# Gathered expert rows kept in program order, six row buffers, and work and memory moved between stages

## Chip, core and metric

The kernel runs on one core of a Trainium2 chip. The metric is device time in microseconds (us), the median of the runs. A core has a matrix engine (PE, with its weight loads PEld), a vector engine (DVE), a scalar engine (ACT), GpSimd (POOL) and a queue engine (SP) that issues most transfers. Each engine works through its own instruction queue in order, and semaphores connect them.

## The reference, cut to what matters

Two model blocks run one after the other on 512 tokens of width 1024, all in float32. The first block is a mixer (a retention branch and a gated spatial branch) followed by a layer of 16384 experts; every token takes 8 heads x 16 experts:

```python
mod = silu(c) @ w_ada + b_ada
x = x + gate1 * (merged @ w_out)             # the mixer
h2 = modulate(rms_norm(x), shift2, scale2)
# per token and head: the 16 best of 16 x 16 candidate experts, g = softmax of their scores
act = gelu(einsum('td,thkd->thk', h2, peer_u[expert])) * g
x = x + gate2 * einsum('thk,thkd->td', act, peer_v[expert])
```

The second block has two layers with window attention, latent attention and a gated convolution, over the 512 tokens and over 256 context tokens. Each layer takes its modulations as `silu(c_2) @ w_mod_2[l]` for the tokens and `silu(c_ctx_2) @ w_mod_2[l]` for the context. The context path of the second block does not depend on the first block.

## The kernel before

Products in float32 are made of three matmuls in a rounded format: each operand is split into a high part (an ACT copy, line 105) and a low part (a subtraction on POOL or DVE, line 107), and `mm3` issues high x high, high x low and low x high (lines 80 to 82).

The stages, in the order of the program:

- `first_mixer`: weights `wA` come through `next_w`, 256 columns at a time. Modulation vectors are products of a matrix with one vector; `matvec` (line 196) does 128 rows of one on DVE, with a 512 KB load of `wm`. `some(n)`, called by `next_w`, takes n such tasks from `mat_tasks`; the list `mw` holds the pool of the `wm` buffers, their number and n. There are 72 tasks: 32 of the first block's modulation and 40 of the context's.
- `experts`: of the 512 tokens the first 384 (`TD`) go through all experts densely. `up_products` makes their 128 products with `eu` (`wr`, `wl`, `u`, `hb`) and stores `hd`; `route` finds the experts and, in its last part (pool `r3`, lines 835 to 868), builds the matrices of gates `gd`; `context` computes the context path of the second block (`cm`, `wrc`, `wlc`). The down-products (lines 594 to 623) go over 32 groups of four rows of `ev`, with `vr` split into `vh` and `vl`, and `ht` times `gt` split into `ah` and `al`; they accumulate in eight banks. They also do the second block's 48 token-modulation matvecs, two per group, from line 618.
- The last 128 tokens go by gathered rows (`gathered`, line 663): 256 steps, each fetching one 128x1024 tile `sg` by an indirect transfer issued on POOL (line 684). 128 steps are dot products with `htok` on DVE (`matvec`, line 197), and 128 add a weighted row to `sacc` (line 699). A head's additions come 16 steps behind its dot products. `sg` has `SG` = 4 buffers; two rows are fetched ahead, and one more before each step. `sacc` is used at line 635, after the down-products.
- `first_out` ends the first block, normalizes and stores `x`; `second` has the two layers.

The other loops carry the up-products and the gathered steps along. `tick(R)` adds R to a counter and takes an up-product for each whole one; `sparse(S)` does the same for gathered steps. `R1`, `R2`, `R3`, `R4` stand for the two parts of routing, the gate matrices and the context; `S3`, `S4`, `SU`, `S5` for the gate matrices (48 calls), the context's `mm` (its calls follow from the loops), the up-products that are left after it, and each row of the down-products (128 calls).

The framework's scheduler sets the final order of each engine's queue. It goes by readiness and a cost model and not by the order of the program alone: an instruction whose operands are ready may be placed ahead of work that stands before it in the code. Buffers of a pool are reused in turn, and a pool that is opened after another was closed may lie on the same memory, from the left side or, with `side="right"`, from the right; its first writes then wait for the last use of what was there.

```python
for _ in range(SG - 2):
    fetch()
for k, (i, j) in enumerate(steps):
    fetch()
    t = rows[k]
```

## Time and profile before

| | us |
|---|---|
| median of 3 runs | 3908.92 |
| lowest, highest | 3907.82, 3917.36 |
| the profiled execution | 3920.43 |
| its span, first to last instruction | 3918.7 |

The mean granted clock of TensorE in the profiled execution is 0.946 of full speed. In the profile, "busy" is time in which an engine executes an instruction; a wait is put down to the work that released it last. An arrow `out<-in` names what an instruction writes and reads. DMA share is the mean busy share of the core's 16 DMA engines, and GB/s is what they moved.

### The profile page before, as it was taken

Reading aid. Unit: us, or ns where it says so; the run is one execution under the profiler, and the core shown is the slowest. Engines: PE = TensorE matmul, PEld = TensorE weight load, DVE = VectorE, ACT = ScalarE, POOL = GpSimd, SP = SyncE. Lnnn points to the kernel's source line nnn. Section 1 sums busy time; section 2 is a strip of 40 time slices with the busy share of each in tenths; the row PEclk is TensorE's granted clock in tenths of the full one; section 3 lists DMA queues with packets and bytes.
Section 4 is the critical chain, followed back from the end, with each engine's and each line's share of the span. In section 5 each row is a group of like instructions: output and inputs, shape, how many; then the busy total and the mean of one; then the engine's idle time right before and its main releaser. Section 6 shows DMA issues by size and latency. Waiting matters only on the chain.

```text
span 3918.7 us, 54792 instructions
## 1 busy us (share of the span) xinstructions
PE 3484.4 (89%) x20243; PEld 3124.0 (80%) x20243; DVE 2363.8 (60%) x4567; ACT 1590.1 (41%) x2976; POOL 1622.9 (41%) x1248
## 2 busy tenths in 40 slices
PE   5999999979878777768999999699999998999998
PEld 4888787878768776767899999687877787777787
DVE  7556545799878786876377555544425554442554
ACT  3322233336633354443433333344426643452563
POOL 4454544451256777675300000155424435543342
PEclk9999999989989887888999999699999998999999
DMA  6346324347888886776789766222221232212113
GB/s 240 132 176 249 124 92 146 107 148 278 295 292 283 315 267 234 274 243 229 257 310 324 244 222 215 77 82 70 66 74 51 89 110 72 71 65 77 50 61 107
DMA packets 271947, 667.91 MB, mean 170 GB/s; under 512 B 25280, under 2 KB 87104, under 8 KB 268736
## 3 DMA queue, kind: packets, MB, share of 16 engines
q1 hardware_dynamic: 219248, 469.30, 35.0%
q0 software_dynamic: 36864, 134.23, 10.1%
q10 hardware_dynamic: 15568, 60.89, 4.1%
q8 instruction: 159, 2.61, 0.3%
q14 instruction: 108, 0.88, 0.1%
HBM read 601.34 MB, written 62.98 MB: 170 GB/s over the span
## 4 chain that ended last, share of the span: by engine, by line
PE 56%; DVE 14%; DMA 10%; issue 9%; POOL 5%; ACT 4%; SPq 0%; POOLq 0%; DVEq 0%; ACTq 0%
PE mm L80 5%; PE mm L81 5%; PE mm L82 5%; PE acc L82 4%; PE acc L81 4%; PE acc L80 4%; PE gm L80 3%; PE gm L81 3%; PE gm L82 3%; DMA sg<-ev,xid 3%; POOL sg L684 2%; PE pv L1083 2%; DMA sg<-ur,xid 2%; POOL wl L107 2%; PE tp L1053 2%
## 5 line engine op out<-in xcount | busy, mean ns | idle before, releaser
L107 POOL TENSOR_TENSOR wl<-wr,wh 128x512 fp32r<-128x512 f32 (+3 forms) x418 | 687.0, 1660 | 472.8 <-ACT wh L105 459.9
L105 ACT CAST wh<-wr 128x512 fp32r<-128x512 f32 (+4 forms) x536 | 348.0, 666 | 512.6 <-PE mm L81 169.7
L80 PE MATMUL u<-hh,wh 128*128 128x384 f32 (+1 forms) x1032 | 369.8, 358 | 34.3 <-ACT hb L711 32.2
L82 PE MATMUL u<-hh,wl 128*128 128x384 f32 (+1 forms) x1032 | 366.2, 355 | 28.6 <-POOL wl L107 16.8
L81 PE MATMUL u<-hl,wh 128*128 128x384 f32 (+1 forms) x1032 | 363.0, 352 | 0.0
L81 PE MATMUL acc<-al,vh 128*128 128x384 f32 (+2 forms) x1056 | 353.1, 335 | 0.1
L82 PE MATMUL acc<-ah,vl 128*128 128x384 f32 (+2 forms) x1056 | 353.0, 335 | 0.0
L80 PE MATMUL acc<-ah,vh 128*128 128x384 f32 (+2 forms) x1056 | 352.8, 335 | 0.0
L105 ACT CAST vh<-vr 128x1024 fp32r<-128x1024 f32 x128 | 134.7, 1052 | 344.3 <-DMA vr<-ev 227.8
L80 PE MATMUL mm<-hh,wh 128*128 128x512 f32 (+2 forms) x608 | 242.0, 401 | 33.1 <-ACT wh L105 23.6
L107 DVE TENSOR_TENSOR vl<-vr,vh 128x1024 fp32r<-128x1024 f32 x128 | 158.5, 1239 | 168.5 <-ACT vh L105 158.8
L684 POOL DMA_INDIRECT sg<-ur,xid x128 | 169.6, 1325 | 213.7 <-DVE sg L197 155.2
L81 PE MATMUL mm<-hl,wh 128*128 128x512 f32 (+2 forms) x608 | 243.2, 400 | 3.3 <-POOL hl L107 3.1
L82 PE MATMUL mm<-hh,wl 128*128 128x512 f32 (+2 forms) x608 | 242.4, 399 | 1.4 <-POOL wl L107 1.4
L80 PEld LDWEIGHTS u<-hh,wh 128*128 128x128 f32 x1032 | 206.9, 201 | 39.0 <-ACT hb L711 34.5
L898 POOL TENSOR_TENSOR acc<-acc,sf 128x256 f32<-128x256 f32 x8 | 6.0, 754 | 558.5 <-ACT sf L895 550.3
L82 PEld LDWEIGHTS u<-hh,wl 128*128 128x128 f32 x1032 | 205.3, 199 | 35.2 <-POOL wl L107 20.2
L197 DVE SCALAR_TENSOR_TENSOR wm<-wm,row 128x1024 f32<-128x1024 f32 x120 | 183.0, 1538 | 72.1 <-DMA wm<-wmod 57.4
L699 DVE SCALAR_TENSOR_TENSOR sacc<-sg,wts,sacc 128x1024 f32<-128x1024 f32 x128 | 189.0, 1476 | 50.4 <-DMA sg<-ev,xid 49.6
L80 PE MATMUL cm<-ch,whc 128*128 128x256 f32 (+1 forms) x584 | 178.0, 306 | 46.0 <-DVE cmt L970 17.5
L684 POOL DMA_INDIRECT sg<-ev,xid x128 | 166.5, 1301 | 125.8 <-DVE sacc L699 84.0
L197 DVE SCALAR_TENSOR_TENSOR sg<-sg,htok 128x1024 f32<-128x1024 f32 x128 | 178.7, 1397 | 59.4 <-DMA sg<-ur,xid 59.3
(726 smaller groups left out, 10256.1 us busy)
## 6 DMA issues: line engine op xcount, KB each, us to landing
wr<-eu SPq DMA_DIRECT2D x256, 256.0 KB, 3.4
vr<-ev SPq DMA_DIRECT2D x128, 512.0 KB, 4.5
wm<-wmod SPq DMA_DIRECT2D x88, 512.0 KB, 5.7
wrc<-w SPq DMA_DIRECT2D x83, 512.0 KB, 5.3
wr<-wA SPq DMA_DIRECT2D x80, 512.0 KB, 4.0
wr<-w SPq DMA_DIRECT2D x156, 256.0 KB, 2.6
wrg<-w SPq DMA_DIRECT2D x104, 256.0 KB, 2.6
hd<-hb ACTq DMA_DIRECT2D x64, 384.0 KB, 4.1
```

What stands on the lines that cost most here:

```text
L80: mm(ps, lh, rh, start=first, stop=False)
L81: mm(ps, lh, rl, start=False, stop=False)
L82: mm(ps, ll, rh, start=False, stop=last)
L105: nc.scalar.copy(hi, x)
L107: eng.tensor_tensor(lo, x, hi.bitcast(F32), op=OP.subtract)
L197: self.nc.vector.scalar_tensor_tensor(chunk, chunk, 1.0, row, op0=OP.mult, op1=OP.mult, accum_out=dst)
L684: nc.gpsimd.indirect_dma_start(t, None, tabs[i], bass.IndirectOffsetOnAxis(idx[:, j:j + 1], 0))
L699: nc.vector.scalar_tensor_tensor(acc, t, wts[:, j:j + 1], acc, op0=OP.mult, op1=OP.add)
L898: eng.tensor_tensor(acc[1], acc[1], sf, op=OP.add)
L1053: nc.tensor.transpose(t[:, (b - i) * 128:(b - i + 1) * 128], p[:, b * 128:(b + 1) * 128], self.ident)
L1083: nc.tensor.matmul(o[:, lo:hi], v(b), pt[k][:, b, lo:hi], start=i == 0 and k == 0, stop=i == len(parts) - 1 and k == 1)
```

## The change

- `here` calls the framework's `keep_in_program_order`: it adds an ordering edge, without a wait, from an instruction to the one that was traced before it on the same engine. Every gathered fetch (POOL) and every gathered step (DVE) gets one.
- `sg` has six buffers instead of four, and three rows are fetched ahead instead of two. The reserved scratch for indirect transfers goes from its default, which is twice as large, to 8192 bytes of each partition, which gives the room.
- The rates change: `R3` 0.7 to 0.6, `R4` 0.38 to 0.45, `S3` 0.6 to 0.8, `S5` 0.85 to 0.75; the call with `S2` = 0 goes.
- The 48 token-modulation matvecs of the second block, with their row `c2`, go from the down-products to `mat_tasks` of the first mixer, which then has 120 tasks; n becomes 3, 4 and 4 in its three parts (2, 2 and 3 before).
- `x` for the down-products and the pool `w2` of the second block's weights lie at the right side, where the up-products' pool was; `x` is loaded after that pool closes. `vr` has three buffers instead of two.

```diff
--- before.py
+++ after.py
@@ -17,7 +17,7 @@
 AX = mybir.AxisListType
 PSUM = bass.MemoryType.PSUM
 
-R1, R2, R3, R4, R5, R6 = 0.6, 0.7, 0.7, 0.38, 0.9, 0.12
+R1, R2, R3, R4, R5, R6 = 0.6, 0.7, 0.6, 0.45, 0.9, 0.12
 PC = 2
 TG, NT = 4, 8
 T = 512
@@ -26,8 +26,8 @@
 ROWS = [(0, 0, 1, 16), (16, 1, 1, 8), (24, 2, 2, 8), (40, 4, 4, 4), (56, 8, 8, 1)]
 HALVES = [(0, 256), (256, 512)]
 TD = 384
-SG = 4
-S2, S3, S4, SU, S5 = 0.0, 0.6, 0.9, 1.2, 0.85
+SG, SD = 6, 3
+S3, S4, SU, S5 = 0.8, 0.9, 1.2, 0.75
 TX = T + TC
 D = 1024
 EPS = 1e-6
@@ -194,7 +194,7 @@
                                            op0=OP.add, op1=OP.subtract)
 
     def matvec(self, chunk, row, dst):
-        self.nc.vector.scalar_tensor_tensor(chunk, chunk, 1.0, row, op0=OP.mult, op1=OP.mult, accum_out=dst)
+        return self.nc.vector.scalar_tensor_tensor(chunk, chunk, 1.0, row, op0=OP.mult, op1=OP.mult, accum_out=dst)
 
     def act_row(self, pool, name, tag="row"):
         row = pool.tile([128, D], F32, name="row", tag=tag, bufs=1)
@@ -214,6 +214,11 @@
             for j in range(n):
                 yield row, self.a["wmod"][l, j], self.mods[l][1][:, j:j + 1]
             self.mod_bias(l, 1, n)
+        row = self.act_row(pool, "c2")
+        for l in range(2):
+            for j in range(24):
+                yield row, self.a["wmod"][l, j], self.mods[l][0][:, j:j + 1]
+            self.mod_bias(l, 0, 24)
 
     def v_(self, name):
         o, n = VOFF[name]
@@ -379,7 +384,7 @@
                         return qk, v
 
                     us = [gate(ps0[2 + c]) for c in range(2)]
-                    mw[:] = self.pool("mr", scope=s3), 2, 2
+                    mw[:] = self.pool("mr", scope=s3), 2, 3
                     ahead_ = project(0)
                     for hd in range(4):
                         dec = rp.tile([128, T], F32, name="dec", tag="dec", bufs=1)
@@ -434,7 +439,7 @@
                             split(z[0][:, cc, :], z[1][:, cc, :], us[c])
                 with ExitStack() as s3:
                     rp = self.pool("rq", 2, scope=s3)
-                    mw[:] = self.pool("mw", scope=s3), 5, 2
+                    mw[:] = self.pool("mw", scope=s3), 5, 4
                     for j in range(4):
                         w = next_w()
                         us = [gate_u(w, c, rp, "u%d" % c)[0] for c in range(2)]
@@ -446,7 +451,7 @@
 
             with ExitStack() as s2:
                 yp_ = self.pool("yg", scope=s2)
-                mw[:] = self.pool("mx", scope=s2), 5, 3
+                mw[:] = self.pool("mx", scope=s2), 5, 4
                 y = (yp_.tile([128, 8, T], F32R, name="yh"), yp_.tile([128, 8, T], F32R, name="yl"))
                 with ExitStack() as s3:
                     vp = self.pool("vn", scope=s3)
@@ -576,15 +581,14 @@
                 self.load(ht, self.hd[g // 2][:, g % 2 * 4:g % 2 * 4 + 4, :])
                 return gt, ht
 
-            x = self.x = vp.tile([128, 8, T], F32, name="x", bufs=1)
             first = inputs(0)
-            self.load(x, self.x1d)
             for _ in units:
                 self.sparse(SU)
             us.close()
+            self.w2 = self.pool("w2", side="right")
+            x = self.x = self.pool("x2", scope=s1, side="right").tile([128, 8, T], F32, name="x")
+            self.load(x, self.x1d)
             ps = ExitStack()
-            row = self.act_row(vp, "c2")
-            todo = [(l, j) for l in range(2) for j in range(24)]
             acc = [self.pool("pacc%d" % c, 1, PSUM, ps).tile([128, T], F32, name="acc%d" % c) for c in range(8)]
 
             def update(c, lo, hi):
@@ -595,7 +599,7 @@
                 gt, ht = first if g == 0 else inputs(g)
                 ops = []
                 for q in range(4):
-                    raw = vp.tile([128, D], F32, name="vr", tag="vr", bufs=2)
+                    raw = vp.tile([128, D], F32, name="vr", tag="vr", bufs=3)
                     self.load(raw, a["ev"][g * 4 + q])
                     vl = vp.tile([128, D], F32R, name="vl", tag="vl", bufs=4)
                     vh = vp.tile([128, D], F32R, name="vh", tag="vh", bufs=4)
@@ -615,13 +619,6 @@
                 if g == 30:
                     for c in range(8):
                         update(c, 0, TD)
-                for l, j in todo[2 * g:2 * g + 2]:
-                    wm = vp.tile([128, D], F32, name="wm", tag="wm", bufs=2)
-                    self.load(wm, a["wmod"][l, j])
-                    self.matvec(wm, row, self.mods[l][0][:, j:j + 1])
-            for l in range(2):
-                self.mod_bias(l, 0, 24)
-
             for _ in self.sunits:
                 pass
 
@@ -659,6 +656,10 @@
         while self.sdue >= 1:
             self.sdue -= 1
             next(self.sunits, None)
+
+    def here(self, ins):
+
+        self.tc.keep_in_program_order(ins)
 
     def gathered(self, idx, gates, ht):
 
@@ -681,22 +682,22 @@
             if len(rows) < len(steps):
                 i, j = steps[len(rows)]
                 t = sp.tile([128, D], F32, name="sg", tag="sg", bufs=SG)
-                nc.gpsimd.indirect_dma_start(t, None, tabs[i], bass.IndirectOffsetOnAxis(idx[:, j:j + 1], 0))
+                self.here(nc.gpsimd.indirect_dma_start(t, None, tabs[i], bass.IndirectOffsetOnAxis(idx[:, j:j + 1], 0)))
                 rows.append(t)
 
-        for _ in range(SG - 2):
+        for _ in range(SD):
             fetch()
         for k, (i, j) in enumerate(steps):
             fetch()
             t = rows[k]
             if i == 0:
-                self.matvec(t, ht, dots[:, j:j + 1])
+                self.here(self.matvec(t, ht, dots[:, j:j + 1]))
                 if j % 16 == 15:
                     js = slice(j - 15, j + 1)
                     nc.scalar.activation(out=wts[:, js], in_=dots[:, js], func=AF.Gelu)
                     nc.vector.tensor_tensor(wts[:, js], wts[:, js], gates[:, js], op=OP.mult)
             else:
-                nc.vector.scalar_tensor_tensor(acc, t, wts[:, j:j + 1], acc, op0=OP.mult, op1=OP.add)
+                self.here(nc.vector.scalar_tensor_tensor(acc, t, wts[:, j:j + 1], acc, op0=OP.mult, op1=OP.add))
             yield
 
     def up_products(self, ws, up, pu):
@@ -782,7 +783,6 @@
                     ti = rp.tile([128, 8, 16], U32, name="ti", tag="ti", bufs=2)
                     for hd in range(8):
                         tick(R2)
-                        self.sparse(S2)
                         self.top16(rp, cand[:, hd], 64, tv[:, hd, :], ti[:, hd, :], "mr2")
                     e = rp.tile([128, 8, 16], F32, name="e", tag="e", bufs=4)
                     nc.vector.tensor_tensor(e, tv, tv[:, :, 0:1].to_broadcast([128, 8, 16]), op=OP.subtract)
@@ -1448,7 +1448,7 @@
         mp = self.pool("m2")
         self.ov = ("ov", 1)
         self.consts2(self.pool("cst2"))
-        ws = (self.pool("w2"), PC, 2, "")
+        ws = (self.w2, PC, 2, "")
         pmm, psc = self.pool("pmm", 1, PSUM), self.pool("psc", 1, PSUM)
 
         def bank(pool, tag, bufs, n=T):
@@ -1813,7 +1813,7 @@
     from concourse.bass_utils import run_bass_kernel_spmd
 
     arrays = layout(inputs)
-    nc = bacc.Bacc("TRN2", target_bir_lowering=False, num_devices=1)
+    nc = bacc.Bacc("TRN2", target_bir_lowering=False, num_devices=1, dynamic_dma_scratch_size=8192)
     a = {n: nc.dram_tensor(n, v.shape, mybir.dt.from_np(v.dtype), kind="ExternalInput").ap() for n, v in arrays.items()}
     out = nc.dram_tensor("out", (128, 8, T), F32, kind="ExternalOutput").ap()
     with tile.TileContext(nc) as tc:
```

## Rows read from the trace of the kernel before

**Rows 1.** The page's part 1, whole span: engine, busy us (share), instructions.
```profile
PE 3484.4 (89%) x20243; PEld 3124.0 (80%) x20243; DVE 2363.8 (60%) x4567; ACT 1590.1 (41%) x2976; POOL 1622.9 (41%) x1248
```

**Rows 2.** By stage: window, length; PE, PEld, DVE, ACT, POOL busy; clock; DMA.
```profile
60.00:260.00 200.00, 185.16 (x1033) 158.52 (x1032) 103.90 (x194) 62.55 (x100) 105.32 (x51) 0.97 0.40 140
260.00:335.00 75.00, 75.00 (x359) 63.27 (x358) 37.26 (x42) 20.25 (x24) 38.00 (x14) 1.00 0.64 227
335.00:535.00 200.00, 186.03 (x985) 160.14 (x985) 116.23 (x175) 55.37 (x80) 105.28 (x48) 0.97 0.50 181
...
865.00:1130.00 265.00, 230.10 (x1690) 212.52 (x1689) 235.72 (x354) 153.50 (x219) 64.33 (x51) 0.93 0.79 280
1130.00:1880.00 750.00, 564.71 (x3564) 533.74 (x3563) 550.46 (x797) 307.84 (x599) 504.45 (x394) 0.87 0.76 261
...
1930.00:2480.00 550.00, 548.16 (x3176) 547.50 (x3176) 346.66 (x496) 193.44 (x276) 11.35 (x9) 0.99 0.74 255
2480.00:2545.00 65.00, 33.50 (x162) 32.24 (x163) 32.98 (x101) 20.30 (x48) 13.78 (x15) 0.53 0.22 78
```

**Rows 3.** One tile, sg and its readers: ns min/median/max, first and last start.
```profile
L699 DVE SCALAR_TENSOR_TENSOR sacc<-sg,wts,sacc x128: 1264/1283/6228, 1001.2 to 1812.6; 128x1024 f32<-128x1024 f32 x128
...
DMA to landing us min/median/max: 4.1/6.3/12.8
```

**Rows 4.** Instruction groups by shape, 1130 to 1880 us.
```profile
L699 DVE SCALAR_TENSOR_TENSOR sacc<-sg,wts,sacc 128x1024 f32<-128x1024 f32 x113 | 169.8, 1503 | 50.4 <-DMA sg<-ev,xid 49.6
L107 POOL TENSOR_TENSOR wl<-wr,wh 128x512 fp32r<-128x512 f32 x96 | 147.0, 1546 | 47.1 <-ACT wh L105 45.8 <-issue 0.6
L684 POOL DMA_INDIRECT sg<-ev,xid x112 | 143.9, 1285 | 65.8 <-DVE sacc L699 42.2 <-issue 12.6 <-DVE sg L197 3.4
L197 DVE SCALAR_TENSOR_TENSOR sg<-sg,htok 128x1024 f32<-128x1024 f32 x96 | 138.8, 1446 | 47.3 <-DMA sg<-ur,xid 47.2
```

**Rows 5.** Waits, 1130 to 1880 us: who for whom, total us, times, longest.
```profile
DVE sacc L699 <- DMA sg<-ev,xid: 49.6, 26, 5.0
DVE sg L197 <- DMA sg<-ur,xid: 47.2, 27, 7.3
...
POOL sg L684 <- DVE sacc L699: 42.2, 26, 3.8
...
POOL sg L684 <- DVE sg L197: 35.7, 20, 5.5
...
PE cm L82 <- DVE wlc L107: 30.1, 22, 7.2
...
PE ct L1053 <- DVE sz L1076: 20.9, 4, 8.4
```

**Rows 6.** Timeline of POOL around 1309 us: start, us, instruction, idle before and releaser.
```profile
1308.97 0.94 POOL L684 DMA_INDIRECT sg<-ev,xid  x1 [2.12 <-DVE sacc L699]
1310.92 4.00 POOL L107 TENSOR_TENSOR wl<-wr,wh 128x512 fp32r<-128x512 f32 x2 [1.02 <-ACT wh L105]
```

**Rows 7.** DMA issues, whole span: count, KB each, median us to landing.
```profile
vr<-ev SPq DMA_DIRECT2D x128, 512.0 KB, 4.5
...
gt<-gd SPq DMA_DIRECT2D x32, 768.0 KB, 6.7
```

**Rows 8.** Instruction groups by shape on DVE, 1930 to 2480 us.
```profile
L197 DVE SCALAR_TENSOR_TENSOR wm<-wm,row 128x1024 f32<-128x1024 f32 x46 | 56.3, 1224 | 31.1 <-DMA wm<-wmod 30.8
```

**Rows 9.** Busy time of one stretch within the down-products.
```profile
2000.00:2100.00 100.00, 100.00 (x579) 100.00 (x578) 75.68 (x114) 33.64 (x46) 0.00 (x0) 1.00 0.92 321
```

**Rows 10.** Instruction groups by shape, 0 to 570 us.
```profile
L197 DVE SCALAR_TENSOR_TENSOR wm<-wm,row 128x1024 f32<-128x1024 f32 x72 | 123.2, 1732 | 22.9 <-DMA wm<-wmod 8.6 <-DMA wm<-wada 7.3 <-POOL wl L107 6.9
```

**Rows 11.** Timeline of the crossing, 2515 to 2545 us.
```profile
2518.56 0.87 DVE L193 SCALAR_TENSOR_TENSOR hl<-nt,md,hh 128x256 fp32r<-128x256 f32 x2
...
2528.53 0.62 ACT L105 CAST kvh<-cl 128x512 fp32r<-128x512 f32 x1 [9.73 <-DMA xd<-x]
...
2537.04 0.58 PE L80 MATMUL mm<-hh,wh 128*128 128x256 f32 x1 [23.57 <-ACT wh L105]
```

## Prediction

> **What bounds the kernel now.** I read the page first: PE is busy 89% of the span, DVE 60%, POOL and ACT 41% [rows 1]. An average over unlike stages, so next the stages [rows 2], cut where the lines of the kernel change: A, first mixer (0 to 605 us); B, routing (to 865); C, gate matrices (to 1130); D, context stage with the last up-products (to 1930, the context itself to 1880); E, down-products (to 2480); F, crossing into the second block (to 2545); G, the rest. The reader is to see that PE is full in E (548 of 550 us) and nearly so in A, but in the 750 us of the context it is busy 565, at a granted clock of 0.87. That is the place with room: 185 us idle, and busy time stretched by the clock.
>
> Third, who fills that stage. All 256 gathered steps are over by 1814 us [rows 3], although the code asks for 106 of them in E (r3 asks 48 times 0.6, the context 109 times 0.9, the last 20 up-products 1.2 each: 150 before it). Of the steps, 113 additions and 96 dot products fall into D [rows 4]; the other 47 came earlier. Their 209 DVE instructions take 309 us of the stage, and DVE stands another 97 us in front of them, waiting for rows to land [rows 5]. DVE is busy 550 of 750 us; with those waits, 647, or 86%. POOL is busy 504 and waits 78 us for DVE to free a row buffer (the two sg rows of POOL) [rows 2, 5]. POOL's queue shows how: a fetch waits 2.1 us for the step just before, and the weight subtraction wl stands behind it [rows 6]. PE pays: 30 us for wlc alone, a subtraction queued on DVE among gathered steps [rows 5]. So in D two in-order queues are clogged by work whose sum is not used before the end of E, while in E POOL does nothing and DVE is idle 203 us.
>
> **The change, part by part.** *Steps held in place.* Each fetch and each step gets an edge to the instruction traced before it on its engine, so none floats ahead. The code then fixes where they go. r3 asks 48 times 0.8 = 38 steps; the context calls its mm 109 times (104 in layer 0, 5 in layer 1) at 0.9 = 98. Up-products: 9.6 + 22.4 + 1 + 48 x 0.6 + 109 x 0.45 = 110 of 128 by then, so 18 remain, with 1.2 each = 22 steps. That is 158 before E; E takes 128 x 0.75 = 96, and 2 are left for the end. D therefore carries 120 steps in place of 209: 89 fewer.
>
> DVE in D: 89 x 1.48 us [rows 4] = 131 us less, 550 - 131 = 419. Landing waits: the code now primes three rows and fetches a fourth before each step, into six buffers; at some 5.5 us between steps a row has over 16 us, against 6.3 us median and 12.8 us maximum from issue to landing [rows 3]. I take 20 of the 97 us as left. POOL: 89 fetches at 1.3 us = 117 less. Up-products move too: r3 does 28.8 instead of 33.6 and so D does 67 instead of 62; five more are 5 x 24 matmuls at 0.173 us (548 us over 3176 in E) = 21 us of PE and 15 us of POOL, cheap beside what leaves. DVE then needs 440, POOL about 430, and PE becomes the longest: 565 us at clock 0.87 is 491 us at full clock, plus 21 = 512. That is the floor. What keeps D above it are the context's own dependent chains, which no row prices apart. I size that by the nearest stage that is clogged less: C, where PE is busy 230 of 265 us (0.87) at clock 0.93. So the context would take 512/0.93/0.87 = 634 in place of 750: **-116**. Bounds: at the share and clock of the mixer between 335 and 535 (0.93 and 0.97) it takes 567, so -183; if half of the landing waits come off and nothing else, -50. What is late next there is PE itself.
>
> C: 7 fewer steps and 5 fewer up-products with their splits on DVE, which is busy 236 of 265: about **-10** (0 to 16).
>
> *E* gets 96 steps and loses 48 matvecs. DVE: 347 - 59 + 96 x 1.3 = 413 of 550 (matvec 1.22 us there [rows 8]). Cover: PE is full and DVE had 203 us free; without it each step would cost its 1.3 us. Transfers: per group four vr, one gt and one ht as large as it, 117 MB in all [rows 7], plus 96 rows of 0.52 MB = 50: 168 MB in 550 us is 305 GB/s, against 142 MB before. One stretch of E moved 321 GB/s with PE at 100% [rows 9], so it fits with 5% to spare. The load of x and the weights of the second block now wait for the up-product buffers, on SP, ahead of vr loads: a 2 MB load at 321 GB/s is 6.5 us. The third vr buffer covers most. **+8** (0 to 40). The two steps left at the end stand before the last updates on DVE: **+2**.
>
> *Modulation in A.* 48 matvecs at 1.73 us [rows 10] = 83 us of DVE, and 25 MB. Calls: 10 x 3, 8 x 4, 16 x 4 instead of 2, 2, 3. DVE has 218 us idle between 60 and 535 us, so it is mostly covered; the tight spot is the output stage (260 to 335): 32 rows and 8 weights are 25.2 MB, at 321 GB/s 79 us against 75, and DVE goes from 37 to 65 of 75. SP meets wm loads that wait for a free buffer, with the wr loads of the next weights behind them; two weights are ahead, 20 us of cover. The silu row moves along, off the start of E. **+10** (0 to 40; all 25 MB exposed would be 78, which the shares of 0.40 to 0.64 speak against).
>
> *Other side of memory.* In F the cosine, mask, key and weight loads start only when x has been stored: ACT waits 9.7 us to 2528.5, and PE 23.6 us to 2537.0, though hh was complete at about 2519 [rows 11]. With x and the second block's first weights apart, their loads can come earlier: **-20** (10 to 26). *Descriptor scratch* halved: nothing, since six rows are in flight (a rival below). S2 was 0.
>
> Sum: 3920.4 - 116 - 10 + 8 + 2 + 10 - 20 = 3794, made against the profiled execution's own 3920.4, 0.3% above the median; by that ratio 3783. I forecast **3785**.
>
> A rule weighed against rows. The dot product on DVE takes 1.45 us in D, where POOL is busy two thirds of the time, and the same form 1.22 in E, where POOL is idle; POOL's wl takes 1.55 us in D [rows 4, 8]. The Trainium skill, "SBUF — State Buffer", section "Who interferes with whom", says that a DVE instruction with two inputs in SBUF and a GpSimd instruction that reads SBUF exclude each other on a shared port. By it the steps moved to E cost 96 x 1.25 rather than 96 x 1.48, and those left in D get cheaper as well, worth perhaps 20 us on either queue of D, an estimate. The rows agree; they, and not the rule, are why I give the larger gain below more than a tenth.
>
> **Rivals.** *The context's own chain sets D* (0.20). For: chain waits of PE such as 20.9 us on sz belong to attention [rows 5], and its matmuls come in series. Then only part of the landing waits goes, D saves 50: 3920 - 50 - 10 - 20 + 20 = 3860, by the median 3850.
>
> *D at PE's floor* (0.15): the context at the mixer's share saves 183, 67 more: 3794 - 67 = 3727, by the median 3715. For: DVE and POOL both fall to some 440 us of 567. Against: the chain waits just named.
>
> *Slower: the rows starve E* (0.07). A step pinned on DVE waits for its row, and vl and al of the next group, which PE needs at once, stand behind. For: 305 of 321 GB/s. Against: six rows in flight cover 34 us. Price: each of the 96 steps stalling 2 us costs 192 us, all on PE; it decides from about 1.3 us per step (126 gained in the other terms, over 96). Then 3975.
>
> *The ring of the halved scratch fills* (0.02): a fetch then waits until an earlier row has landed, 6.3 us rather than 1.3, 5.0 x 120 in D alone: 600 us, 4380. "SBUF — State Buffer" of the Trainium skill, section "SBUF size: 192, 224, or 256?", says that the 16 KiB hold the descriptor rings of such transfers. No run here shows the ring full.
>
> *It does not do what it says* (0.04): edges go only to the one instruction traced before, which may itself float; the steps still end before E, and A's cost eats F's gain: 3905.
>
> **How the numbers follow.** The forecast case has 0.52: 3740 to 3825. A measurement of this kernel can tell about 0.3%, 12 us, from no change. Faster are the forecast, the chain and the floor, 0.87, and a part of the last rival: 0.88; within 0.3%: 0.05; slower 0.07 (starved E and full ring, less the milder ends that stay below). The range reaches to both neighbouring cases: 3700 to 3885.
>
> **What would show it.** Right: the last sacc step starts near 2470, 95 or so steps fall into E; the DVE and POOL sg waits of D together fall from 175 us below 50; the context is 90 to 140 us shorter with a clock over 0.9; PE stays above 97% in E; F's first matmul follows hh within a few us; A is at most 15 us longer. Wrong: D as long with DVE less busy (the chain), PE idle in E under sg waits (starved rows), or A longer by 30 us under wr landings.

## The result and the profile after

The changed kernel took 3776.56 us, median of 4 runs (3773.70 to 3785.09), against 3910.68 for the kernel before, median of 4 runs beside it: ratio 0.9658, 95% interval 0.9638 to 0.9678, a gain of 134 us. The forecast was 3785 us, the ratio to its starting point 0.968. A second series on another chip gave 3771.85 (ratio 0.9621, 0.9599 to 0.9643).

The profiled execution after spans 3771.9 us (3918.7 before). The page's part 1, as in [rows 1]:

```profile
PE 3453.4 (92%) x20243; PEld 3099.7 (82%) x20243; DVE 2364.8 (63%) x4557; ACT 1583.2 (42%) x2972; POOL 1616.1 (43%) x1258
```

PE, DVE and POOL do the same work as before. So the gain is not less work but work in another place, and it has to be read by stages. The stages of the prediction were cut at fixed times, which no longer fit; from here on they are cut by events, the same in every kernel. A ends with the first matmul into `uq` (routing), B with the first matmul into `gps`, C with the last one; "context" runs from there to the first addition into `cot`, where layer 0 of the context merges; D ends with the last `hb`, E with the last `acc` matmul of the dense tokens, F and G are the rest. B is 303 to 307 us in all kernels and is left out below. In us, from the profiled executions:

| kernel | A | C | D (context) | E | F, G | median | ratio (95%) |
|---|---|---|---|---|---|---|---|
| before | 588.9 | 232.2 | 824.8 (702.0) | 552.1 | 1416.2 | 3910.68 | 1 |
| changed | 622.9 | 204.0 | 700.6 (567.1) | 548.5 | 1389.8 | 3776.56 | 0.9658 (0.9638 to 0.9678) |
| changed, again | 624.6 | 203.5 | 698.9 (563.7) | 551.6 | 1385.3 | 3771.85 | 0.9621 (0.9599 to 0.9643) |
| e1 no edges | 621.8 | 200.3 | 809.2 (708.6) | 551.3 | 1388.5 | 3878.88 | 0.9889 (0.9870 to 0.9907) |
| e2 edges alone | 588.7 | 216.9 | 721.9 (580.9) | 627.7 | 1415.1 | 3874.86 | 0.9881 (0.9864 to 0.9899) |
| e3 four rows | 626.8 | 209.7 | 716.5 (578.0) | 548.6 | 1389.3 | 3780.29 | 0.9640 (0.9611 to 0.9670) |
| e4 modulation in E | 594.5 | 206.2 | 700.5 (565.5) | 603.1 | 1383.9 | 3795.76 | 0.9673 (0.9653 to 0.9693) |
| e5 left side | 624.2 | 207.4 | 703.5 (568.4) | 551.1 | 1414.3 | 3807.85 | 0.9710 (0.9690 to 0.9731) |
| e7 150 steps in E | 625.1 | 208.9 | 647.5 (530.1) | 558.0 | 1386.3 | 3727.60 | 0.9503 (0.9483 to 0.9524) |
| e8 mixer in order | 656.0 | 207.0 | 701.3 (567.4) | 550.1 | 1384.4 | 3809.35 | 0.9729 (0.9700 to 0.9759) |
| e9 half of it later | 605.8 | 207.8 | 700.9 (567.7) | 549.5 | 1398.2 | 3774.70 | 0.9630 (0.9607 to 0.9652) |
| e10 four wm | 590.7 | 202.0 | 701.5 (570.2) | 588.0 | 1383.4 | 3782.41 | 0.9661 (0.9628 to 0.9694) |
| e11 169 steps in E | 621.2 | 204.4 | 642.1 (522.2) | 562.0 | 1389.1 | 3724.38 | 0.9498 (0.9469 to 0.9526) |
| e12 two in output | 617.3 | 208.5 | 642.1 (520.3) | 558.4 | 1383.5 | 3719.79 | 0.9493 (0.9476 to 0.9510) |

Ratios are to runs of the kernel before on the same chip. The two profiles of the changed kernel differ by up to 5 us in a stage; a smaller difference between two kernels says nothing here.

Changed less before, stage by stage: A +34.0, B +1.6, C -28.2, D -124.2, E -3.6, F and G -26.4, together -146.8, the difference of the spans. The stretches that answer [rows 2] and, for C and the context, cover the stages (columns as there):

```profile
260.00:335.00 75.00, 64.49 (x269) 51.86 (x269) 54.91 (x74) 14.27 (x17) 28.85 (x11) 0.91 0.77 290
335.00:535.00 200.00, 180.29 (x971) 155.70 (x970) 150.97 (x217) 53.63 (x74) 108.59 (x44) 0.96 0.70 247
929.00:1133.00 204.00, 176.90 (x1433) 161.63 (x1433) 192.99 (x307) 134.32 (x179) 57.84 (x38) 0.97 0.83 298
1133.00:1700.00 567.00, 510.48 (x3484) 493.53 (x3482) 379.00 (x567) 292.30 (x568) 344.00 (x280) 0.95 0.70 238
1834.00:2382.00 548.00, 545.04 (x3165) 544.59 (x3163) 410.15 (x581) 199.01 (x294) 105.33 (x103) 0.98 0.85 297
```

C and the context of the kernel before, cut by the same events:

```profile
893.40:1125.60 232.20, 203.16 (x1556) 187.51 (x1554) 204.93 (x322) 141.18 (x195) 53.16 (x42) 0.94 0.82 291
```

```profile
1126.00:1828.00 702.00, 520.58 (x3289) 491.52 (x3288) 527.56 (x735) 287.23 (x553) 487.08 (x378) 0.87 0.78 269
```

In the context PE is now busy 510 of 567 us (90%) at clock 0.95; before, it was busy 521 of 702 (74%) at 0.87, for 195 matmuls fewer. DVE went from 528 to 379 us there, POOL from 487 to 344. E is as full of PE as it was, with DVE up and the transfers at 0.85. The bad lines are those of A: between 260 and 335 us PE was busy 75 of 75 us, and now 64; in the 200 us behind that, 186, and now 180.

Where the gathered additions stand (tile `sg`, as [rows 3]), and their groups on DVE in the context, as in [rows 4]:

```profile
L700 DVE SCALAR_TENSOR_TENSOR sacc<-sg,wts,sacc x128: 1255/1278/3548, 1020.0 to 2353.3; 128x1024 f32<-128x1024 f32 x128
```

```profile
L700 DVE SCALAR_TENSOR_TENSOR sacc<-sg,wts,sacc 128x1024 f32<-128x1024 f32 x47 | 73.3, 1559 | 3.9 <-DMA sg<-ev,xid 3.9
L197 DVE SCALAR_TENSOR_TENSOR sg<-sg,htok 128x1024 f32<-128x1024 f32 x48 | 68.8, 1434 | 10.5 <-DMA sg<-ur,xid 10.5
```

The last addition moved from 1812.6 to 2353.3 us, 29 us before the end of E. The context has 95 steps on DVE; it had 210. The waits there, as [rows 5]:

```profile
DVE wlc L107 <- ACT whc L105: 79.0, 48, 7.9
...
POOL sg L685 <- DVE sg L197: 20.2, 9, 5.8
...
POOL sg L685 <- DVE sacc L700: 15.3, 5, 6.3
...
DVE sg L197 <- DMA sg<-ur,xid: 10.5, 6, 3.0
...
PE cm L82 <- DVE wlc L107: 8.3, 8, 3.6
```

The clog of the context is gone: POOL waits 36 us for rows to be freed (78 before), DVE 14 us for rows to land (97 before), PE 8 us for `wlc` (30 before). What tops the list now is DVE waiting for ACT, idle time of an engine that is busy 379 of 567 us, where PE is busy 510.

The crossing, as [rows 11]: start, duration, instruction.

```profile
2397.01 0.56 PE L80 MATMUL pv<-hh,whg 128*128 128x256 f32 x1
```

```profile
2397.05 1.31 ACT L192 ACTIVATE hh<-nt,md 128x256 fp32r<-128x256 f32 x3 [5.39 <-DVE nt L191]
...
2406.09 0.33 ACTq L75 DMA_DIRECT2D xd<-x  x1
```

Products of the second block run while the later columns of `hh` are still being written, and 9 us before the store of `x` is issued; before, PE stood idle for 23.6 us, up to 2537.0, 8.5 us after that store had landed [rows 11].

### The profile page after: what moved, and what is told of

Its sections match the earlier page's. It is cut to its first block, busy times and chain, and to the rows that moved or that the text cites. A ratio compares the mean times of both kernels' runs of the same rounds, so it can differ in the third digit from the quotient of the medians.

```text
span 3771.9 us, 54793 instructions
## 1 busy us (share of the span) xinstructions
PE 3453.4 (92%) x20243; PEld 3099.7 (82%) x20243; DVE 2364.8 (63%) x4557; ACT 1583.2 (42%) x2972; POOL 1616.1 (43%) x1258
## 4 chain that ended last, share of the span: by engine, by line
PE 45%; DVE 4%; ACT 2%; DMA 2%; POOL 2%; issue 2%; SPq 0%; POOLq 0%; ACTq 0%; DVEq 0%
PE acc L81 5%; PE acc L82 5%; PE acc L80 5%; PE gm L80 4%; PE gm L81 3%; PE gm L82 3%; PE mm L80 3%; PE mm L81 3%; PE mm L82 3%; PE pv L1083 2%; PE tp L1053 2%; PE sc L80 1%; PE sc L82 1%; PE sc L81 1%; POOL wl L107 1%
## 5 line engine op out<-in xcount | busy, mean ns | idle before, releaser
L107 POOL TENSOR_TENSOR wl<-wr,wh 128x512 fp32r<-128x512 f32 (+3 forms) x428 | 705.1, 1665 | 522.8 <-ACT wh L105 489.5
L80 PE MATMUL acc<-ah,vh 128*128 128x384 f32 (+2 forms) x1056 | 353.1, 336 | 14.5 <-DMA vr<-ev 13.2
L685 POOL DMA_INDIRECT sg<-ur,xid x128 | 150.0, 1172 | 295.5 <-DVE sg L197 277.6
L197 DVE SCALAR_TENSOR_TENSOR wm<-wm,row 128x1024 f32<-128x1024 f32 x120 | 201.7, 1707 | 42.5 <-DMA wm<-wada 15.8
L80 PEld LDWEIGHTS acc<-ah,vh 128*128 128x128 f32 x1056 | 202.6, 192 | 15.3 <-issue 13.5
L81 PEld LDWEIGHTS acc<-al,vh 128*128 128x128 f32 x1056 | 203.0, 192 | 4.8 <-DVE al L107 4.8
L81 PEld LDWEIGHTS u<-hl,wh 128*128 128x128 f32 x1032 | 204.9, 199 | 0.9 <-issue 0.2
L82 PEld LDWEIGHTS acc<-ah,vl 128*128 128x128 f32 x1056 | 202.9, 192 | 0.0
```

Source lines behind the costliest of these rows:

```text
L80: mm(ps, lh, rh, start=first, stop=False)
L81: mm(ps, lh, rl, start=False, stop=False)
L82: mm(ps, ll, rh, start=False, stop=last)
L107: eng.tensor_tensor(lo, x, hi.bitcast(F32), op=OP.subtract)
L197: return self.nc.vector.scalar_tensor_tensor(chunk, chunk, 1.0, row, op0=OP.mult, op1=OP.mult, accum_out=dst)
L685: self.here(nc.gpsimd.indirect_dma_start(t, None, tabs[i], bass.IndirectOffsetOnAxis(idx[:, j:j + 1], 0)))
```

## Experiments

**e1: the whole change, but the edges.** Theory: the edges alone make D's gain. Rival: the extra buffers and the rates make it.

```diff
     def here(self, ins):
-        self.tc.keep_in_program_order(ins)
+        return ins
```

> The changed kernel without the ordering edges on the gathered fetches and steps; six buffers, three rows ahead, rates, moved modulation and memory sides stay. Theory of the prediction (the steps leave the context stage because the edges hold them back): the steps float again, all 256 are done before the down-products' first vl, the context stage (from the last gate matmul to the last up-product, 701 us changed, 825 before) grows to 790 to 850, and the time is 3860 to 3930. Rival (the six row buffers and three rows ahead do it, wherever the steps stand): the landing waits stay small and the time is 3776 to 3800.

Slower than the changed kernel by 2.4% (0.9889 over 0.9658), and all of it in D, 809.2 us; A, C, E and F stay as changed. The theory holds. The last addition is back at 1795.4 us. The context of e1, its steps, and the waits of DVE for rows:

```profile
1126.40:1835.00 708.60, 554.28 (x3480) 527.65 (x3478) 548.79 (x744) 295.77 (x573) 512.35 (x400) 0.87 0.79 278
```

```profile
L700 DVE SCALAR_TENSOR_TENSOR sacc<-sg,wts,sacc 128x1024 f32<-128x1024 f32 x116 | 188.2, 1623 | 14.7 <-DMA sg<-ev,xid 14.3
L197 DVE SCALAR_TENSOR_TENSOR sg<-sg,htok 128x1024 f32<-128x1024 f32 x100 | 146.8, 1468 | 20.0 <-DMA sg<-ur,xid 19.9
```

```profile
DVE sg L197 <- DMA sg<-ur,xid: 19.9, 10, 5.2
DVE sacc L700 <- DMA sg<-ev,xid: 14.3, 16, 1.8
```

This run tells two suspects apart, the steps and the waits in front of them. Its context makes the same products as the changed kernel's (3480 and 3484 matmuls), and the waits are small in both: DVE waits 34 us for rows here and 14 there, POOL 24 and 36 us for buffers. What differs is the number of steps, 216 for 95, and the context takes 709 us for 567. So the steps that DVE and POOL execute cost the time. What the longer waits of the kernel before cost ([rows 5]) this run does not show cleanly: its context is as long as that one, 709 against 702 us, but with 191 matmuls more in it, and PE is idle 154 us for 181.

**e2: the kernel before, with the edges alone.**

```diff
-                nc.gpsimd.indirect_dma_start(t, ...)
+                self.here(nc.gpsimd.indirect_dma_start(t, ...))
-                self.matvec(t, ht, dots[:, j:j + 1])
+                self.here(self.matvec(t, ht, dots[:, j:j + 1]))
-                nc.vector.scalar_tensor_tensor(acc, ...)
+                self.here(nc.vector.scalar_tensor_tensor(acc, ...))
```

> The kernel before with the ordering edges alone; four buffers, two rows ahead, old rates, modulation and x where they were. Theory of the prediction: the context stage shortens by about 100 us of its 825; the down-products then carry 106 gathered rows and the 48 modulation rows, 117 + 56 + 25 = 198 MB, at 322 GB/s 615 us against 552 before, so they lose some 60; the time is 3840 to 3890. Rival (buffers do it): the time stays within 15 us of the kernel before.

The edges take 103 us from D and give back 76 in E. The two halves of E, and who waited in it (waits of ACT, e2 first, the changed kernel below):

```profile
1880.00:2130.00 250.00, 224.13 (x1197) 209.43 (x1197) 196.21 (x289) 70.82 (x99) 42.61 (x42) 0.99 0.94 348
2130.00:2380.00 250.00, 238.26 (x1336) 232.44 (x1335) 176.49 (x236) 81.87 (x114) 50.47 (x48) 0.99 0.84 301
```

```profile
ACT vh L105 <- DMA vr<-ev: 386.1, 112, 13.9
```

```profile
ACT vh L105 <- DMA vr<-ev: 24.7, 5, 8.9
```

With two `vr` buffers and the matvecs in E, 112 rows of `ev` land late, and PE is idle 26 us of the first 250. Neither half makes the gain: against the same runs of the kernel before, e1 saves 41 us and e2 45; the whole change saves 134. So it takes the rest of the change to let E carry the steps; e4 has three `vr` buffers and still pays 55.

**e3: four row buffers, two rows ahead.**

```diff
-SG, SD = 6, 3
+SG, SD = 4, 2
```

> The changed kernel with four row buffers and two rows fetched ahead, as before the change; the edges stay. Theory (the edges do it): a fetch still stands two to three steps ahead of its step, 11 us or more at the 5.5 us between steps, against 6 us from issue to landing; D (700 us after the change) grows by at most 15 us, E stays at 548 to 556: 3772 to 3792 us. Rival (the pinned steps need the two extra rows): every late row now stops DVE, some 2 us for each of the 109 steps of D and of the 96 of E; D 740 or more, E 600 or more: 3850 us and above.

D is 16 us longer and E the same; by median e3 can't be told from the changed kernel (the profile is of its slowest run, 18 us above its median). In the context DVE and POOL wait 118 us for rows and buffers, 50 in the changed kernel; with as many matmuls (3483) and as many steps it takes 11 us more. So 68 us more of such waits came with only some 11 us of time. The rival falls: pinned steps do not need the two extra rows at 96 steps in E.

**e4: the modulation back in the down-products.** The 48 matvecs return to E, with n at 2, 2, 3; `vr` keeps three buffers.

```diff
+                for l, j in todo[2 * g:2 * g + 2]:
+                    wm = vp.tile([128, D], F32, name="wm", tag="wm", bufs=2)
+                    self.load(wm, a["wmod"][l, j])
+                    self.matvec(wm, row, self.mods[l][0][:, j:j + 1])
...
```

> The changed kernel with the second block's 48 modulation matvecs back in the down-products (and 2, 2, 3 tasks per weight in the mixer). Theory A (the move pays because transfers are the limit of the down-products, 322 GB/s in the changed kernel): the mixer gets its 34 us back, the down-products have 168 + 25 = 193 MB and grow from 548 to about 600 us; the time is 3790 to 3815. Rival B (the down-products have room for both, PE full): the time falls by the mixer's 34 us, to about 3742.

A gives back 28 us, E grows by 55. The time is the one that theory A gave; whether the transfers are its reason, e7 tells. Waits in E of DVE and of SP's queue, and E in two parts (the matvecs end in the first):

```profile
DVE wm L197 <- DMA wm<-wmod: 67.1, 16, 7.9
...
SPq L72 <- DVE wm L197: 102.5, 16, 10.3
```

```profile
1815.00:2115.00 300.00, 265.42 (x1427) 259.01 (x1426) 229.58 (x336) 89.58 (x124) 55.38 (x48) 0.95 0.92 342
2115.00:2365.00 250.00, 250.00 (x1444) 250.00 (x1444) 186.41 (x249) 88.90 (x124) 45.41 (x45) 1.00 0.91 319
```

DVE stands in front of a matvec whose row has not landed, with `vl` and `al` of the next group behind it; SP stands in front of a `wm` load without a buffer, with `vr` loads behind it. The first part loses 35 us of PE, at 342 GB/s. That these queues are what makes E longer is argued here; e10 tests a part of it.

**e5: x and the second block's weights back at the left side.**

```diff
+            x = self.x = vp.tile([128, 8, T], F32, name="x", bufs=1)
             first = inputs(0)
+            self.load(x, self.x1d)
...
-        ws = (self.w2, PC, 2, "")
+        ws = (self.pool("w2"), PC, 2, "")
```

> The changed kernel with x and the second block's weights where they were before (x in the down-products' pool and loaded before the last up-products, weights in a pool at the left). Theory of the prediction: only the crossing changes; the time from the last down-product to the end goes back from 1390 to about 1414 us, the down-products stay within 5 us of 549, and the time is 20 to 27 us above the changed kernel. Rival (the crossing's gain is the rates' or the modulation's, since first_out no longer waits for other work): within 5 us of the changed kernel.

F and G return to 1414 us, no other stage moves by more than 5 us, and the waits of [rows 11] come back: ACT 9.7 us for `kvh` (9.7 before), PE 23.0 us for its first `mm` (23.6 before). The theory holds, though the time is 36 us above the changed kernel run beside it, more than the 20 to 27 expected; F and G account for 24 to 29 of them.

**e7: more steps in E.**

```diff
-S3, S4, SU, S5 = 0.8, 0.9, 1.2, 0.75
+S3, S4, SU, S5 = 0.8, 0.5, 1.2, 1.1
```

> The changed kernel with S4 = 0.5 and S5 = 1.1: some 44 gathered steps fewer in the context stage and as many more in the down-products (150 of 256). Theory T (transfers bound the down-products: 322 GB/s at a DMA share of 0.92 in the changed kernel): they need 117 + 150 x 0.52 = 196 MB, 608 us, so they grow by 50 to 65 us; the context stage gains 0 to 30, and the time is 25 to 60 us above the changed kernel. Rival P (PE bounds them, DVE and transfers have room): they stay at 549 to 560 and the context stage gains 20 to 50: below the changed kernel.

This beat the changed kernel, run beside it, by 44 us: theory T falls, and the rival holds. 142 steps stand in E and 54 in the context. The context, and 450 us of E:

```profile
1139.00:1669.00 530.00, 497.37 (x3482) 482.56 (x3481) 303.34 (x503) 291.56 (x568) 281.46 (x243) 0.97 0.65 217
1830.00:2280.00 450.00, 450.00 (x2589) 450.00 (x2588) 379.76 (x514) 161.54 (x225) 137.21 (x123) 1.00 0.99 366
```

PE does not stop once at 366 GB/s. The 321 GB/s of [rows 9], which the prediction took for a ceiling, was only what that kernel asked for. It also clears the bytes in e4: 117 MB and 142 rows of 0.52 MB are 191 MB here in 558 us; 117 MB with 96 rows and 25 MB of `wm` are 192 MB there in 603.

**e8: the mixer's loads in program order.** Edges on the `wm` and `wr` loads of A, so that no later `wm` load passes a weight.

```diff
-                        self.load(wm, t[1])
+                        self.here(self.load(wm, t[1]))
...
-            self.load(r, src[:, k:k + c, :])
+            i = self.load(r, src[:, k:k + c, :])
+            if self.mixing:
+                self.here(i)
```

> The changed kernel with ordering edges also on the wm and wr loads of the first mixer, so that SP's queue has 3 or 4 modulation rows, then one weight, throughout. Theory S (the mixer's 34 us come from the order in SP's queue: 16 wm loads stand ahead of the next weight at 267 to 293 us and ACT waits 19 us for it): most of the output stage's 15 us come back, the mixer shortens by 12 to 25 us, and the time is 3750 to 3765. Rival D (it is the 25 MB or the 83 us of DVE as such): the mixer stays within 6 us, the time 3770 to 3785.

A grew by another 33 us. SP's waits in A, e8 first, the changed kernel below:

```profile
SPq L73 <- DVE wm L200: 240.6, 75, 34.4
```

```profile
SPq L72 <- DVE wm L197: 164.9, 80, 10.9
```

In program order SP waits longer for `wm` buffers, and the weights can no longer pass. In the output stage the order does what the theory says: the products on `zh` take 75.5 us from the first to the last, as before the change, and 89.9 in the changed kernel. But they begin 30 us later, and what follows them takes 18 us more. The remedy fails, neither forecast came, and what is shown is that SP's order is worth tens of us in A.

**changed kernel again**, the control of the second series.

> The changed kernel itself once more, for comparisons on one chip: 0.966 of the kernel before; stages as in its first profile (mixer 623, context stage 701, down-products 549 us) within 5 us each.

**e9: the 24 matvecs of layer 1 moved out of A**, into layer 0 of the second block; `late_mod` takes one at each `tick` there. n is 3, 2, 4.

```diff
+        def late_mod():
+            mv = self.pool("mv2", scope=s2)
+            row = self.act_row(mv, "c2")
+            for j in range(24):
+                wm = mv.tile([128, D], F32, name="wm", tag="wm", bufs=1)
+                self.load(wm, a["wmod"][1, j])
+                self.matvec(wm, row, self.mods[1][0][:, j:j + 1])
+                yield
...
```

> The changed kernel with the second layer's 24 modulation matvecs done in the second block's first layer, beside its latent attention, and 3, 2 and 4 tasks per weight in the mixer, so that the output stage has 16 modulation rows as before the change. Theory S (the mixer lost 34 us because modulation rows crowd out weights in SP's queue in the output stage, and fill DVE after it): the mixer shortens to 600 to 608 us, the second block, with transfers at 0.2 of their time and DVE half idle, lengthens by at most 5 us; the ratio to the kernel before is 0.959 to 0.963. Rival D (each modulation row costs its DVE time wherever it stands): 24 x 1.7 = 41 us come back at the second block's cost, the ratio stays within 0.003 of the changed kernel's.

A gives back 19 us (one profile), as the theory had it, but F and G cost 13 where it allowed 5; the median doesn't move. Why they cost 13 there stays open.

**e10: e4 with four `wm` buffers**, and four rows to make room (e3 is its control). Against e4:

```diff
-SG, SD = 6, 3
+SG, SD = 4, 2
...
-                    wm = vp.tile([128, D], F32, name="wm", tag="wm", bufs=2)
+                    wm = vp.tile([128, D], F32, name="wm", tag="wm", bufs=4)
```

> The kernel with the token modulation back in the down-products (E was 603 us there), now with four wm buffers instead of two; to make room sg has four buffers, as in the run beside it. Theory W (the two buffers): in E the matvecs stopped DVE 67 us for wm rows, with vl and al behind them, and SP stood 94 us before wm loads that wait for a buffer, with vr loads behind; with four buffers E falls to 550 to 565, total 3745 to 3765 plus what four rows cost. Rival T (the bytes): 168 MB and 25 MB of wm in E are the limit; then E stays at 595 to 610 and the total at 3790 to 3805. The kernel with 150 steps in E moved as many bytes in 558 us, which speaks against T.

```profile
DVE wm L197 <- DMA wm<-wmod: 39.2, 17, 7.6
...
SPq L72 <- DVE wm L197: 19.7, 5, 11.8
```

Both waits fall, from 67 to 39 and from 102 to 20 us, and E from 603 to 588. By its profile the buffers are a part of e4's 55 us, not most of it; by median e10 can't be told from e4 (0.9661 and 0.9673). E is still 40 us over. PE is idle for 27 us of it, for 3 in the changed kernel, and stands 23 us in front of `al`, a subtraction in DVE's queue; its busy time is 16 us longer. Whether the late `wm` rows ahead of `al` are the reason stays open.

**e11: still more steps in E**: 168 there, 27 in the context.

```diff
-S3, S4, SU, S5 = 0.8, 0.9, 1.2, 0.75
+S3, S4, SU, S5 = 0.8, 0.25, 1.2, 1.4
```

> S4 0.25 and S5 1.4: 27 calls' worth of steps in the context instead of 98, about 169 steps in E instead of 96 (150 in the last run of this kind). E then moves 117 MB and 169 rows of 0.52 MB, 206 MB: 373 GB/s in 552 us. Theory (E still has room, DVE first to end it: 169 x 1.3 + 294 us of its own work is 514 of 552): E 552 to 565, D 620 to 630, total 3700 to 3715 us. Rival (370 GB/s, the most that E moved over several stretches, is the limit): vr lands late and PE waits in E, E 580 or more, total 3735 to 3765, no better than 150 steps.

```profile
1136.00:1658.00 522.00, 493.53 (x3485) 479.47 (x3484) 265.69 (x474) 286.00 (x562) 231.58 (x212) 0.98 0.56 188
1860.00:2260.00 400.00, 399.12 (x2301) 398.47 (x2300) 359.52 (x490) 140.73 (x195) 174.33 (x134) 1.00 1.03 396
```

E feeds PE at 396 GB/s over 400 us. D yields 5 us more than in e7 (642 us, where 620 to 630 were expected), E takes 4 of them: by ratio the two are equal. E's rival, a limit at 370 GB/s, falls.

**e12: e11, with n at 4, 2, 4 in the mixer.** The same 120 tasks, 16 of them out of the output stage.

```diff
-                    mw[:] = self.pool("mr", scope=s3), 2, 3
+                    mw[:] = self.pool("mr", scope=s3), 2, 4
...
-                    mw[:] = self.pool("mw", scope=s3), 5, 4
+                    mw[:] = self.pool("mw", scope=s3), 5, 2
```

> S4 0.25 and S5 1.4 as in the run of 169 steps in E (3724 us), and the mixer's n is 4, 2, 4 instead of 3, 4, 4: the same 120 tasks, with two instead of four at each of the 8 calls of the output stage, where 16 wm loads stood on SP ahead of the next wr and the zh products took 90 us instead of 75. Theory S (what costs in A is wm loads ahead of weights in that stage): the zh products take 75 to 77 us again, the part before them up to 6 us more than now, A 608 to 616 instead of 621; B to G as in that run; total 3709 to 3719. Rival (120 tasks cost DVE and SP the same wherever they stand): A 620 to 632, total 3722 to 3735.

A from 60 to 335 us; e11 first, e12 below:

```profile
60.00:260.00 200.00, 182.26 (x1006) 154.80 (x1005) 117.52 (x213) 62.24 (x101) 103.46 (x50) 0.96 0.45 157
260.00:335.00 75.00, 63.01 (x267) 50.88 (x266) 58.97 (x74) 13.91 (x16) 28.05 (x11) 0.91 0.78 285
```

```profile
60.00:260.00 200.00, 175.15 (x954) 150.45 (x953) 126.42 (x218) 59.20 (x96) 101.42 (x47) 0.91 0.52 179
260.00:335.00 75.00, 75.00 (x334) 61.87 (x334) 39.10 (x56) 17.20 (x22) 35.36 (x14) 1.00 0.66 225
```

The output stage is full again: its products on `zh` take 75.5 us for 90.4. But they begin 12.6 us later, and the stretch before them loses 7 us of PE. A falls by 4 us, no more than two profiles of one kernel differ in a stage, and ends, as the time does, between the theory and its rival: the place was found, but most of the cost moves along with the loads.

## Why the prediction was right, and where its terms were off

**D, -116 forecast, -124 measured.** The mechanism holds: without edges the gain is gone (e1), with edges alone it is there (e2, -103). 95 steps stand in the context (the rates give 104 x 0.9 = 94 to its layer 0), 96 in E, and the clock rose to 0.95. One sign did not come: the sg waits of DVE and POOL, 175 us before, fell to 50 in the context but to 90 over all of D, and under 50 was named. The size was taken over from C, a share of 0.87 and a clock of 0.93; the context came to 0.90 and 0.95. What the argument had wrong is the weight of the waits. It counted 97 us of landing waits beside 131 us of instructions; e3 has 68 us more waits on DVE and POOL together and loses some 11.

What pays is steps: in the context 216 to 95 saves 141 us (e1 to the changed kernel, 1.17 each), 95 to 54 saves 37 (0.90 each, e7), 54 to 27 saves 8 (0.30 each, e11). The price of a step falls as PE fills the stage, 78, 90, 94 and 95% busy, and in E, where PE is full, the 46 and 72 steps that e7 and e11 add cost 6 to 13 us, 0.1 to 0.2 each. So the chain of the context (0.20) did not decide, and the floor (0.15) came within reach only when still more steps left. One figure does not follow from its terms: POOL's 504 us less 117 and plus 15 are 402, not 430. Nothing rests on it; POOL was busy 344 of 567 us.

**C, -10 forecast (0 to 16), -28 measured.** The term was sized by DVE alone. PE's busy time fell by 26 us in C, from 203.2 to 176.9, because 123 matmuls of the up-products left it, the very 21 us that the prediction added to D and did not take from C. e1 has the same C without edges, so the edges are not needed for it; the rates, which send the up-products elsewhere, were not run alone. Edges alone take 15 us off C (e2), with 29 steps in it for 42.

**A, +10 forecast (0 to 40), +34 measured.** Inside its bounds, but beyond the 15 us that were to show it right, and the sign that was named for it being wrong came: `wr` lands late in the output stage. Its 64 high-by-high products on `zh`, before and after:

```profile
L80 PE MATMUL mm<-zh,wh x64: 389/389/389, 252.1 to 327.5; 128*128 128x512 f32 x64
```

```profile
L80 PE MATMUL mm<-zh,wh x64: 387/389/397, 258.5 to 348.4; 128*128 128x512 f32 x64
```

The first starts 6.4 us later than before, the last 20.9 us later, so 6 us are lost ahead of the stage, 14.5 in it and 13 behind it, where DVE is busy 151 of 200 us for 116 [rows 2]. SP's timeline in the stage, then ACT's:

```profile
266.89 26.51 SPq L72 DMA_DIRECT2D wm<-wmod  x16
293.49 0.86 SPq L72 DMA_DIRECT2D wr<-wA  x2
```

```profile
299.98 2.22 ACT L105 CAST wh<-wr 128x1024 fp32r<-128x1024 f32 x2 [18.96 <-DMA wr<-wA]
```

Sixteen `wm` loads stand ahead of the next weight for 26.5 us, more than the 20 us of cover that the prediction gave to two weights ahead; ACT then waits 19 us. That cover is the step that failed: it was not held against a row of loads in SP's queue. The 14.5 us are this row's: with half the `wm` loads there (e9, e12) or in program order (e8) the products on `zh` take 75.5 us again. But only in e9, which took 24 matvecs out of A, is A shorter by more than 4 us: e12 loses 13 us ahead of the stage, e8 30 ahead of it and 18 behind. All in all a matvec in A costs 0.6 to 0.8 us (28 us for 48 in e4, 19 for 24 in e9), and what sets that price outside the output stage is not shown.

**E, +8 forecast, -4 measured; end +2.** Right: PE busy 545 of 548 us, 96 steps in it:

```profile
L700 DVE SCALAR_TENSOR_TENSOR sacc<-sg,wts,sacc 128x1024 f32<-128x1024 f32 x56 | 71.5, 1277 | 0.0
...
L197 DVE SCALAR_TENSOR_TENSOR sg<-sg,htok 128x1024 f32<-128x1024 f32 x40 | 48.7, 1218 | 4.2 <-DMA sg<-ur,xid 4.2
```

The rival of starved rows (0.07) is refuted: DVE waits 4 us for rows in E, and even 168 steps do not starve it (e11). Its premise, 305 of 321 GB/s, was a demand read as a limit. To take the modulation out of E paid all the same, though not for its bytes (e7): e4 gets 28 us back in A and pays 55 in E, and by the ratios that part of the change gains 6 to 20 us. The last addition starts 29 us before the end of E; the 2470 us that the prediction named stood on the old times, in which E ends at 2502.5.

**F, -20 forecast, -26 measured**, and e5 returns it: the memory sides alone make it. **The ring** (0.02): POOL issues a fetch in 1.3 us in the context, as before [rows 4], and in 1.0 in E (92 records, 95 us); nothing in these runs shows it full.

**The rule that was weighed.** A step costs 1.22 and 1.28 us in E, where POOL is busy 105 of 548 us, and 1.43 and 1.56 in the context, where POOL is busy 61% of the time. Steps moved to E did get cheaper, as the row of before and the Trainium skill's "SBUF — State Buffer", section "Who interferes with whom", have it; no run changes POOL's work alone, so that it is the reason is not shown. Those left behind did not get cheaper: with POOL down from 69% to 61% they cost what they did [rows 4]. The 20 us that the prediction estimated for them are not there.

The terms sum to -126 in the forecast and -147 in the profile: C and F gave 24 us more, D 8 and E with the end 14, and A took 24 back. That the median came within 9 us of the forecast is in part luck: A's miss was covered by what the others gave beyond theirs.

## What to carry to other kernels

Work whose result is needed late, but whose operands are ready early, may be placed early by a scheduler that goes by readiness, as all 256 steps were here; look for it in the queues of a stage that is not full of PE, and pin it to the stage where PE is full and the other engines are idle. Size such a move by the instructions removed from the clogged queues and by PE's floor, not by the waits that they show, which cost far less here than they measure (e3). A transfer rate read off a trace is a demand until a run that asks for more fails to get it, and loads placed on a shared queue are to be priced as a whole row of them ahead of the one that is needed (26.5 us here).

## What the runs showed of the hardware

One core's transfers reached 396 GB/s over 400 us with PE full (e11), where the prediction had taken 321 GB/s for the ceiling; in the same stretch the DMA share reads 1.03, so that column is no hard scale near its top. Two pages of the Trainium skill differ on this: "DMA: Bandwidth & Descriptors", section "Where 436 GB/s comes from", has transfers between HBM and SBUF bound at about 358 GB/s for a core, while "Perfetto Trace Analysis", section "Roofline", lets a single active core pull more than that share, up to about 435. These runs agree with the second. TensorE's granted clock in the context went from 0.87 to 0.95 and to 0.98 as its idle time fell from 181 us to 57 and 28 (before, changed, e11), so the fuller stage had the higher clock as well.
